# A 32 MB copy on 16 DMA engines: streams 1920 KB apart in place of 2 MB

## The chip, the core and the metric

The kernel runs on one core of one Trainium2 chip. The metric is the device time of the program in microseconds (us). A profile of one execution shows the span from the first to the last instruction, what each engine did in it, and the packets of the core's 16 DMA engines. In this text KB and MB in code and in address distances are 1024 and 1024 x 1024 bytes; MB and GB/s in the profile are decimal.

## The reference

```python
batch, seq, hidden, capacity = 16, 1024, 512, 256
x = randn(batch, seq, hidden)                      # float32, 32 MB
token_positions = randint(0, capacity, (batch, seq))

mask = token_positions < capacity
return (x * mask[..., np.newaxis]).astype(np.float32)
```

A row of 512 numbers is kept if its token's position is below the capacity, else it becomes zero. The positions are drawn below the capacity, so with these inputs every row is kept, and the output equals x. The kernel doesn't assume that: it tests the positions and has a branch for the other case.

## The kernel before

The kernel starts at once to copy x to out, from HBM to HBM, with transfers that SP (the sync engine) issues. The tensor is cut into 16 streams of 2 MB, one for each DMA engine. Each transfer takes the next stretch of every stream: 64 KB, then 192 KB, then seven times 256 KB.

```python
KB = 1024 // 4          # in float32 elements

x_e = x_b.rearrange("(e c) -> e c", e=16)
out_e = out_b.rearrange("(e c) -> e c", e=16)
c = 64 * KB
at = 0
for n in [1, 3] + [4] * 7:
    sp.dma_start(
        out=out_e[:, at : at + n * c], in_=x_e[:, at : at + n * c]
    ).then_inc(s_copy, 16)
    at += n * c
    n_copy += 1
```

Beside the copy, the positions are loaded through ACT's queue; the vector engine (DVE) compares them with the capacity, a matmul on TensorE (PE) adds up the kept rows of all partitions, and one more comparison gives a flag.

```python
act.dma_start(out=tp, in_=tp_i32.rearrange("(p w) -> p w", p=P)).then_inc(s_tp, 16)
# ... five DVE instructions: ge, lt, low, keep, kept ...
pe.matmul(out=total, lhsT=ones, rhs=kept, start=True, stop=True).then_inc(s_pe, 1)
ve.tensor_scalar(out=drop_i, in0=total, scalar1=float(N) - 0.5,
                 scalar2=None, op0=Alu.is_lt).then_inc(s_ve, 1)
```

If the flag says that a row is to be dropped, a branch multiplies x by the mask tile by tile and writes out again, after the copy is done. With these inputs the branch isn't taken. The last instruction of SP waits until all the transfers have landed:

```python
with nc.If(drop):
    ...                                   # not taken with these inputs
sp.wait_ge(s_copy, 16 * n_copy)
```

Of the kernel before, what the change touches and what calls it, by code (L numbers as in the profile page):

```python
# [1 line left out]

# [4 lines left out]


@with_exitstack
def kernel(  # L10
    ctx: ExitStack,
    tc: tile.TileContext,
    x: bass.AP,
    token_positions: bass.AP,
    capacity: bass.AP,
    out: bass.AP,
):
    nc = tc.nc
    P = nc.NUM_PARTITIONS
    fp32 = mybir.dt.float32  # L20
    i32 = mybir.dt.int32
    Alu = mybir.AluOpType

    x_f = x.flatten_outer_dims()
    out_f = out.flatten_outer_dims()
    N, D = x_f.shape
    n_per_p = N // P
    cap = float(int(capacity))
    x_r = x_f.rearrange("(p n) d -> p n d", p=P)
    out_r = out_f.rearrange("(p n) d -> p n d", p=P)  # L30
    tp_i32 = token_positions.rearrange("b s -> (b s)").bitcast(i32)

    sp = nc.sync
    act = nc.scalar
    ve = nc.vector
    pe = nc.tensor

    pool = ctx.enter_context(tc.tile_pool(name="mask", bufs=1))
    psum_pool = ctx.enter_context(tc.tile_pool(name="psum", bufs=1, space=bass.MemoryType.PSUM))
    tp = pool.tile([P, 2 * n_per_p], i32, name="tp")  # L40
    ge = pool.tile([P, n_per_p], fp32, name="ge")
    lt = pool.tile([P, n_per_p], fp32, name="lt")
    low = pool.tile([P, n_per_p], fp32, name="low")
    keep = pool.tile([P, n_per_p], fp32, name="keep")
    kept = pool.tile([P, 1], fp32, name="kept")
    ones = pool.tile([P, 1], fp32, name="ones")
    total = psum_pool.tile([1, 1], fp32, name="total")
    drop_i = pool.tile([1, 1], i32, name="drop_i")
    F = 16
    NBUF = 2  # L50
    n_fix = n_per_p // F
    xts = [pool.tile([P, F, D], fp32, name=f"xt{b}") for b in range(NBUF)]

    s_copy = tc.alloc_semaphore("s_copy")
    s_tp = tc.alloc_semaphore("s_tp")
    s_ve = tc.alloc_semaphore("s_ve")
    s_pe = tc.alloc_semaphore("s_pe")
    s_ld = [tc.alloc_semaphore(f"s_ld{b}") for b in range(NBUF)]
    s_mul = tc.alloc_semaphore("s_mul")
    s_st = [tc.alloc_semaphore(f"s_st{b}") for b in range(NBUF)]  # L60

    with tc.tile_critical():  # L62

        n_copy = 0
        x_b = x_f.rearrange("r d -> (r d)")
        out_b = out_f.rearrange("r d -> (r d)")

        def copy(eng, first, count, view, **sizes):
            eng.dma_start(
                out=out_b[first : first + count].rearrange(view, **sizes),  # L70
                in_=x_b[first : first + count].rearrange(view, **sizes),
            ).then_inc(s_copy, 16)

        KB = 1024 // 4
        MB = 1024 * KB

        x_e = x_b.rearrange("(e c) -> e c", e=16)
        out_e = out_b.rearrange("(e c) -> e c", e=16)
        c = 64 * KB
        at = 0  # L80
        for n in [1, 3] + [4] * 7:
            sp.dma_start(
                out=out_e[:, at : at + n * c], in_=x_e[:, at : at + n * c]
            ).then_inc(s_copy, 16)
            at += n * c
            n_copy += 1
        assert 16 * at == N * D


        act.dma_start(out=tp, in_=tp_i32.rearrange("(p w) -> p w", p=P)).then_inc(s_tp, 16)  # L90
        lo = tp[:, 0 : 2 * n_per_p : 2]
        hi = tp[:, 1 : 2 * n_per_p : 2]


        ve.memset(ones, 1.0).then_inc(s_ve, 1)  # L95
        ve.wait_ge(s_tp, 16)
        ve.tensor_scalar(  # L97
            out=ge, in0=lo, scalar1=0.0, scalar2=None, op0=Alu.is_ge
        ).then_inc(s_ve, 1)
        ve.wait_ge(s_ve, 2)  # L100
        ve.scalar_tensor_tensor(  # L101
            out=lt, in0=lo, scalar=cap, in1=ge, op0=Alu.is_lt, op1=Alu.mult
        ).then_inc(s_ve, 1)
        ve.wait_ge(s_ve, 3)
        ve.scalar_tensor_tensor(  # L105
            out=low, in0=hi, scalar=0.0, in1=lt, op0=Alu.is_equal, op1=Alu.mult
        ).then_inc(s_ve, 1)
        ve.wait_ge(s_ve, 4)
        ve.scalar_tensor_tensor(  # L109
            out=keep, in0=hi, scalar=0.0, in1=low, op0=Alu.is_lt, op1=Alu.add  # L110
        ).then_inc(s_ve, 1)
        ve.wait_ge(s_ve, 5)
        ve.tensor_reduce(  # L113
            out=kept, in_=keep, axis=mybir.AxisListType.X, op=Alu.add
        ).then_inc(s_ve, 1)
        pe.wait_ge(s_ve, 6)
        pe.matmul(out=total, lhsT=ones, rhs=kept, start=True, stop=True).then_inc(s_pe, 1)  # L117
        ve.wait_ge(s_pe, 1)
        ve.tensor_scalar(  # L119
            out=drop_i, in0=total, scalar1=float(N) - 0.5, scalar2=None, op0=Alu.is_lt  # L120
        ).then_inc(s_ve, 1)


        for e in (sp, act, ve):
            e.wait_ge(s_ve, 7)
        ET = mybir.EngineType
        drop = nc.values_load(
            drop_i[0:1, 0:1],
            engines=[ET.SP, ET.Activation, ET.DVE],
            min_val=0,  # L130
            max_val=1,
            skip_runtime_bounds_check_because="a comparison gives 0 or 1",
        )
        with nc.If(drop):
            for u in range(n_fix):
                b = u % NBUF
                if u >= NBUF:
                    sp.wait_ge(s_st[b], 16 * (u // NBUF))
                sp.dma_start(out=xts[b], in_=x_r[:, u * F : (u + 1) * F, :]).then_inc(s_ld[b], 16)
                ve.wait_ge(s_ld[b], 16 * (u // NBUF + 1))  # L140
                for j in range(F):
                    c = u * F + j
                    ve.tensor_scalar(
                        out=xts[b][:, j, :],
                        in0=xts[b][:, j, :],
                        scalar1=keep[:, c : c + 1],
                        scalar2=None,
                        op0=Alu.mult,
                    ).then_inc(s_mul, 1)
                if u == 0:  # L150
                    act.wait_ge(s_copy, 16 * n_copy)
                act.wait_ge(s_mul, (u + 1) * F)
                act.dma_start(out=out_r[:, u * F : (u + 1) * F, :], in_=xts[b]).then_inc(s_st[b], 16)
            for b in range(NBUF):
                act.wait_ge(s_st[b], 16 * (n_fix // NBUF))
        sp.wait_ge(s_copy, 16 * n_copy)


# [1 line left out]
_INS = ['x', 'token_positions', 'capacity']  # L160
_OUTS = [((16, 1024, 512), 'float32')]

_NUMBERS = {'capacity': 256}


# [26 lines left out]
```

## Time and profile before

| | |
|---|---|
| time, median of 2 runs | 172.03 us (170.79 to 173.28) |
| span in the profile | 170.1 us |
| busy time of DVE, the busiest compute engine | 1.6 us |
| moved by the copy | 33.55 MB read, 33.55 MB written |
| transfers of the copy | 9, in packets of 64 KB |

A packet is a piece that one DMA engine moves[...]; the profile gives the number of packets of each queue, their bytes, and the time that they took as a share of what 16 engines have in the span. Queue q1 carries the transfers that SP issued, q10 those of ACT. A view of windows gives the mean busy share of the 16 engines and the bytes moved, stretch by stretch. Each transfer ends with one small completion packet on each engine that took part; these count in the number of packets.

### The profile page before, as it was taken

What the parts mean: (1) busy time and instruction counts of PE and PEld (TensorE: products, weight loads), DVE (VectorE), ACT (ScalarE), POOL (GpSimd) and SP (SyncE); (2) the same over time, 40 slices, a digit from 0 to 9 for tenths busy, and PEclk for the clock granted to TensorE, in tenths of its full rate; (3) what the DMA queues carried; (4) which work ended last, traced back from release to release, by engine and by line L of the source; (5) the groups of instructions that cost most, each with busy time, mean ns of one, the idle gap of its engine ahead of it and who ended that gap; (6) DMA issues with size and microseconds to landing.
All of it is one profiled execution on the core that took longest, in us unless ns stands there. A gap on an engine that the chain in (4) does not pass through costs nothing. (4 is left out here: it accounts for less than half of the span.)

```text
span 170.1 us, 82 instructions
## 1 busy us (share of the span) xinstructions
PE 0.2 (0%) x2; PEld 0.1 (0%) x2; DVE 1.6 (1%) x7; POOL 0.2 (0%) x4
## 2 busy tenths in 40 slices
PE   0000000000000000000000000000000000000000
PEld 0000000000000000000000000000000000000000
DVE  2100000000000000000000000000000000000000
POOL 0000000000000000000000000000000000000000
DMA  9949999879999949999969999979999499999570
GB/s 277 200 92 216 233 247 231 185 154 185 231 247 247 216 92 231 200 247 231 185 123 216 231 247 200 200 154 200 231 247 231 92 216 200 247 247 231 108 154 0
DMA packets 801, 33.69 MB, mean 198 GB/s; under 512 B 160, under 2 KB 288, under 8 KB 288
## 3 DMA queue, kind: packets, MB, share of 16 engines
q1 hardware_dynamic: 656, 33.56, 96.4%
q10 hardware_dynamic: 144, 0.13, 0.2%
q14 instruction: 1, 0.01, 0.0%
HBM read 33.69 MB, written 33.55 MB: 395 GB/s over the span
## 5 line engine op out<-in xcount | busy, mean ns | idle before, releaser
L101 DVE SCALAR_TENSOR_TENSOR lt<-tp,ge 128x128 f32<-128x128 int32 x1 | 0.3, 293 | 0.0
L109 DVE SCALAR_TENSOR_TENSOR keep<-tp,low 128x128 f32<-128x128 int32 x1 | 0.3, 293 | 0.0
L105 DVE SCALAR_TENSOR_TENSOR low<-tp,lt 128x128 f32<-128x128 int32 x1 | 0.3, 291 | 0.0
L113 DVE TENSOR_REDUCE kept<-keep 128x1 f32<-128x128 f32 x1 | 0.3, 286 | 0.0
L97 DVE TENSOR_SCALAR ge<-tp 128x128 f32<-128x128 int32 x1 | 0.2, 226 | 2.0 <-DMA tp<-in_token_positions_dram 2.0
L117 PE MATMUL total<-kept,ones 128*1 128x1 f32 x2 | 0.2, 164 | 4.6 <-DVE kept L113 4.6
L119 DVE TENSOR_SCALAR drop_i<-total 1x1 int32<-1x1 f32 x1 | 0.1, 147 | 0.3 <-PE total L117 0.3
L173 POOL MEMSET const-uint8-127<- 128x1 uint8 x1 | 0.1, 103 | 0.0
L173 POOL MEMSET const-bfloat16-1.0<- 128x1 bf16 x1 | 0.1, 101 | 0.0
L173 POOL MEMSET const-float32-0.0<- 128x1 f32 x1 | 0.1, 98 | 0.2 <-issue 0.2
L173 POOL MEMSET const-float32-1.0<- 128x1 f32 x1 | 0.1, 98 | 0.0
L117 PEld LDWEIGHTS total<-kept,ones 128*1 128x1 f32 x2 | 0.1, 80 | 4.6 <-DVE kept L113 4.6
L95 DVE MEMSET ones<- 128x1 f32 x1 | 0.1, 59 | 1.0 <-SPq L62 1.0
## 6 DMA issues: line engine op xcount, KB each, us to landing
out_dram<-in_x_dram SPq DMA_DIRECT2D x9, 82.2
tp<-in_token_positions_dram ACTq DMA_DIRECT2D x1, 128.0 KB, 2.1
```

Of the source, the lines that this page charges most:

```text
L95: ve.memset(ones, 1.0).then_inc(s_ve, 1)
L97: ve.tensor_scalar(out=ge, in0=lo, scalar1=0.0, scalar2=None, op0=Alu.is_ge).then_inc(s_ve, 1)
L101: ve.scalar_tensor_tensor(out=lt, in0=lo, scalar=cap, in1=ge, op0=Alu.is_lt, op1=Alu.mult).then_inc(s_ve, 1)
L105: ve.scalar_tensor_tensor(out=low, in0=hi, scalar=0.0, in1=lt, op0=Alu.is_equal, op1=Alu.mult).then_inc(s_ve, 1)
L109: ve.scalar_tensor_tensor(out=keep, in0=hi, scalar=0.0, in1=low, op0=Alu.is_lt, op1=Alu.add).then_inc(s_ve, 1)
L113: ve.tensor_reduce(out=kept, in_=keep, axis=mybir.AxisListType.X, op=Alu.add).then_inc(s_ve, 1)
L117: pe.matmul(out=total, lhsT=ones, rhs=kept, start=True, stop=True).then_inc(s_pe, 1)
L119: ve.tensor_scalar(out=drop_i, in0=total, scalar1=float(N) - 0.5, scalar2=None, op0=Alu.is_lt).then_inc(s_ve, 1)
L173: nc = _bacc.Bacc("TRN2", target_bir_lowering=False, num_devices=1)
```

## The change

The 16 streams start 1920 KB apart, where they were 2 MB apart, and each is 1920 KB long. They cover the first 30 MB of the tensor: 64 KB, 192 KB, six times 256 KB, and 128 KB of each stream. The last 2 MB of the tensor are copied by one further transfer, again cut into 16 parts, of 128 KB each. What it is for: DMA engines that start together and move at the same pace stand at equal offsets within their streams, so their addresses differ by multiples of the streams' distance; another distance gives other combinations of addresses in HBM at any moment.

```diff
-        x_e = x_b.rearrange("(e c) -> e c", e=16)
-        out_e = out_b.rearrange("(e c) -> e c", e=16)
-        c = 64 * KB
+        E = 16
+        PITCH = 1920 * KB
+        x_e = x_b[0 : E * PITCH].rearrange("(e c) -> e c", e=E)
+        out_e = out_b[0 : E * PITCH].rearrange("(e c) -> e c", e=E)
         at = 0
-        for n in [1, 3] + [4] * 7:
+        for c in [64, 3 * 64] + [4 * 64] * 6 + [2 * 64]:
             sp.dma_start(
-                out=out_e[:, at : at + n * c], in_=x_e[:, at : at + n * c]
+                out=out_e[:, at : at + c * KB], in_=x_e[:, at : at + c * KB]
             ).then_inc(s_copy, 16)
-            at += n * c
+            at += c * KB
             n_copy += 1
-        assert 16 * at == N * D
+        assert at == PITCH
+        copy(sp, E * PITCH, N * D - E * PITCH, "(e c) -> e c", e=E)
+        n_copy += 1
```

The function `copy` issues one transfer of a stretch of x to the same stretch of out and lets it add 16 to `s_copy`. As built, the last transfer has 32 rows of 64 KB.

## The prediction

> **What bounds the kernel now.** I read the page from its top: first the line of busy times, to see whether any engine computes for a noticeable part of the span; then the queues; then the waits of the queue that issues the copies; and last the rate in windows of 10 us, because a mean over the span hides its ends.
>
> The head of the page and the part on DMA queues:
>
> ```profile
> span 170.1 us, 82 instructions
> PE 0.2 (0%) x2; PEld 0.1 (0%) x2; DVE 1.6 (1%) x7; POOL 0.2 (0%) x4
> ...
> q1 hardware_dynamic: 656, 33.56, 96.4%
> q10 hardware_dynamic: 144, 0.13, 0.2%
> ...
> HBM read 33.69 MB, written 33.55 MB: 395 GB/s over the span
> ```
>
> No compute engine is busy for more than 1.6 us of 170.1. The queue q1, which SP feeds, holds packets on the 16 DMA engines for 96.4% of the span. So the copy from x to out is the kernel. The 656 packets of q1 can be checked: 32 MB in pieces of 64 KB are 512, and 9 transfers with one completion packet on each of 16 engines are 144; 512 + 144 = 656. So every transfer does use 16 engines, and each engine moves 512 / 16 = 32 pieces.
>
> Next the waits of SP's queue (who waited, for whom, how long in total, how often, the longest), and the copies' issues in the merged timeline (start, duration, engine, line):
>
> ```profile
> SPq L156 <- DMA out_dram<-in_x_dram: 160.6, 1, 160.6
> ...
> 0.95 6.37 SPq L82 DMA_DIRECT2D out_dram<-in_x_dram  x9
> ...
> 4.83 0.15 DVE L119 TENSOR_SCALAR drop_i<-total 1x1 int32<-1x1 f32 x1 [0.28 <-PE total L117]
> ```
>
> All nine transfers are issued between 0.95 and 7.32 us, after that SP waits 160.6 us for their bytes. The test of the mask is over at 4.98 us, under the first pieces of the copy. The view of the chain that ended last lists only these first 5 us and a DMA share of 1%: it follows the mask back and doesn't show the copy, so it is not the view to read here; the 160.6 us wait is.
>
> Then the windows (stretch, length, four engines' busy time, granted clock, mean DMA share, GB/s written), the first, three from the middle and the last:
>
> ```profile
> 0.00:10.00 10.00, 0.19 (x2) 0.09 (x2) 1.59 (x7) 0.20 (x4) 1.00 1.06 223
> ...
> 60.00:70.00 10.00, 0.00 (x0) 0.00 (x0) 0.00 (x0) 0.00 (x0) 1.00 1.06 216
> 70.00:80.00 10.00, 0.00 (x0) 0.00 (x0) 0.00 (x0) 0.00 (x0) 1.00 0.90 184
> 80.00:90.00 10.00, 0.00 (x0) 0.00 (x0) 0.00 (x0) 0.00 (x0) 1.00 0.85 164
> ...
> 160.00:171.00 11.00, 0.00 (x0) 0.00 (x0) 0.00 (x0) 0.00 (x0) 1.00 0.45 89
> ```
>
> The fifteen windows from 10 to 160 us read 211, 210, 203, 210, 210, 216, 184, 164, 203, 210, 203, 197, 216, 203, 210; they sum to 3050, so the mean is **203.3 GB/s** (a packet is counted whole in one window, so single values jump). At that rate 33.55 MB take 33.55 / 0.2033 = 165.0 us. The remaining 170.1 - 165.0 = 5.1 us are what doesn't depend on the rate: the first data packet starts at 2.4 us by the packet records of the trace, and the rest is the uneven finish of the engines (the sixteen completions of the last transfer come at 165.1 to 168.8 us) and the closing of the program. The median time is 172.03, that is 1.9 us above the span. So **time = 7.0 us + 33.55 MB / rate**, and the change can act on the rate alone.
>
> One more reading, from the packet records: one 64 KB piece took 5.12 us on average, with 3.61 as the shortest and 6.69 as the longest. The shortest, in the first round, is 18.2 GB/s for one engine, and 16 times that would be 290 GB/s. Hence one engine by itself can go faster than the 12.8 GB/s (65,536 bytes / 5.12 us) that it gets; what holds it back seems to be something that the 16 share. That is the opening for a change of addresses.
>
> **What the Trainium skill says.** DMA: Bandwidth & Descriptors, section Latency and other measured facts, has a row on the pitch of HBM rows: copies between HBM tensors in tiles of 128 rows of 16 KiB ran at 207 GB/s with rows 512 KiB apart, 164 with 2 MiB, 103 with 4 and 8 MiB, and 214 ("full") with 4 MiB padded by 4 KiB. It calls channel aliasing of streams in lock-step an inference. Does the trace agree? Streams here are 2 MB apart and yet reach 203.3, not 164: either few streams suffer less than 128 rows, or the neighbours in time on that page are the first rows of each engine's share. If an engine takes 8 neighbouring rows, its stream there starts 8 x 512 KiB = 4 MiB from the next engine's in the 207 case and 16 MiB in the 164 case; a spacing of 2 MB would then lie on the good side of 207. The trace's 203.3 fits this second reading, which is my choice.
>
> HBM Reference, section Specifications, says that a core alone measures about 425 GB/s. Reads and writes together, the trace has 2 x 203.3 = 407 GB/s in the steady part. If that figure holds for the sum of both directions, which no run here shows, there is room for 425 / 407 = 1.045.
>
> DMA: Bandwidth & Descriptors, section on why a DMA increments its semaphore by 16, says that the number of engines is the largest divisor up to 16 of the slowest dimension. The 656 packets agree for a dimension of 16. The new last transfer is built as 32 rows of 64 KB, which 16 divides, so it should use 16 engines too, with two pieces each.
>
> **The change part by part.**
> 1. *Pieces and bytes.* Before: 1 + 3 + 7 x 4 = 32 pieces of 64 KB for each engine. After: 1 + 3 + 6 x 4 + 2 = 30, which is 1920 KB, and 2 from the last transfer: again 32. No packet gets smaller. 0 us.
> 2. *One transfer more.* Ten in place of nine: 16 completion packets more, one per engine; each lasts 9 ns in the packet records. One issue more on SP: 6.37 / 9 = 0.71 us, at about 7.3 us, when the first transfers keep the engines occupied to 25.1 us (last completion of the second). Hidden. Together under 0.05 us.
> 3. *Mask, branch, PE, DVE.* Same instructions, over at 5 us. 0 us.
> 4. *The order of addresses.* At any moment the engines stand at one offset inside their streams, give or take. Before, the sixteen addresses are equal except in multiples of 2 MB. After, 1920 KB = 2 MB - 128 KB, so each stands 128 KB further back within its 2 MB block, and sixteen engines stand at sixteen different multiples of 128 KB. This is the whole purpose, and covers 30 of 32 pieces; in the last two the streams are 128 KB apart. It doesn't separate anything below 128 KB.
>
> So the sum is 7.0 + 33.55 / rate. Rate 203.3 (nothing gained): 7.0 + 165.0 = 172.0. Rate 207: 7.0 + 162.1 = 169.1. Rate 214 (the page's "full"): 7.0 + 156.8 = 163.8. All are estimates from the formula of the trace and the named page.
>
> **The rivals.**
> *A: the 2 MB spacing costs nothing today, and the time stays.* For it: 203.3 GB/s is not far from the page's 207 and far from 164; and the engines are not in exact lock-step. In every round the sixteen starts lie about 3 us apart, which at 12.8 GB/s is 38 KB of address, more than the 4 KiB that cured the case on the page. So the streams may be spread already. Against it: the short first-round piece shows a shared limit, and the pieces scatter from 3.6 to 6.7 us. Time 171 to 173.
> *B: the streams do collide now, and part of the gap to 214 is recovered.* For it: the page's row, and 5.0% between 203.3 and 214. Against: the same drift of 38 KB. Time 164 to 168.5.
> *C: the new spacing collides more.* No trace or page shows which address bits choose a channel; 1920 KB is still a multiple of 128 KB, and sixteen addresses that move one field up while another goes down may fall together as well as apart. A rate of 195 would give 7.0 + 172.1 = 179. Against: nothing here makes this spacing look special.
> *D: a tail.* The last 2 MB could land unevenly or on fewer engines. With 32 rows it shouldn't; two pieces per engine are 10 us of the end whichever way they are addressed. Worth 1 us at most.
>
> **Range and chances.** I give A a half, B somewhat more than a third, C an eighth or so. The middle of that mixture is just below the time before: 170.3 us. The range runs from nearly full recovery, 164.5, to a slight loss, 175.0. The 2% limits stand at 168.6 and 175.5; B lies mostly below the first, C partly above the second: faster 0.35, same 0.53, slower 0.12.
>
> **What would show each step.** The page after should have q1 with 512 + 160 = 672 packets and the same 33.56 MB; more data packets would break step 1. The issue group of SP should still end by 9 us, with the mask over at 5. Windows from 10 to 160 us near 203 mean A; 207 to 214 in all of them mean B; below 200 C. If the middle windows rise and the last 10 us get slower, D took it back. The formula itself is wrong if the time moves by more than the windows say. The prediction fails upward if the spacing makes collisions that it didn't have, downward if the shared limit was the collision and the ceiling is above the page's 214.

## The result, and the profile after

The changed kernel takes **108.84 us** (median of 2 runs, 108.81 to 108.86) against 172.03: a ratio of 0.633, 95% interval 0.613 to 0.652. That is far below the predicted range; the time fell by 63 us.

Lines of the page after, in the same order as those shown of before: span and busy engines, queues, bytes.

```profile
span 107.0 us, 83 instructions
PE 0.2 (0%) x2; PEld 0.1 (0%) x2; DVE 1.6 (1%) x7; POOL 0.2 (0%) x4
...
q1 hardware_dynamic: 672, 33.56, 95.5%
...
HBM read 33.69 MB, written 33.55 MB: 628 GB/s over the span
```

The same bytes, 512 data packets and 10 x 16 completion packets, the same 1.6 us of DVE, and the DMA engines as fully occupied as before (95.5% against 96.4%). That share says nothing of how fast the packets move: it adds up the times that packets took, however long each one lasts. The figure that moved is the last one, 395 to 628 GB/s (read and written together).

SP's waits and issues after, in the order of before:

```profile
SPq L159 <- DMA out_dram<-in_x_dram: 97.4, 1, 97.4
```

```profile
0.95 5.87 SPq L83 DMA_DIRECT2D out_dram<-in_x_dram  x9
6.87 0.59 SPq L69 DMA_DIRECT2D out_dram<-in_x_dram  x1
```

The tenth issue ends at 7.46 us, hidden as expected. The wait for the bytes is 97.4 us where it was 160.6: a difference of 63.2 us, the whole gain. The windows (stretch, length, busy times, clock, DMA share, GB/s written), and last the mean over the middle:

```profile
0.00:10.00 10.00, 0.19 (x2) 0.09 (x2) 1.59 (x7) 0.20 (x4) 1.00 1.00 328
...
60.00:70.00 10.00, 0.00 (x0) 0.00 (x0) 0.00 (x0) 0.00 (x0) 1.00 1.08 354
70.00:80.00 10.00, 0.00 (x0) 0.00 (x0) 0.00 (x0) 0.00 (x0) 1.00 0.96 315
80.00:90.00 10.00, 0.00 (x0) 0.00 (x0) 0.00 (x0) 0.00 (x0) 1.00 1.02 334
...
100.00:108.00 8.00, 0.00 (x0) 0.00 (x0) 0.00 (x0) 0.00 (x0) 1.00 0.37 131
10.00:100.00 90.00, 0.00 (x0) 0.00 (x0) 0.00 (x0) 0.00 (x0) 1.00 1.00 326
```

The copy is faster in every window, from the first on; nothing is special to the end. Over 10 to 100 us the mean is 326 GB/s, where it was 203. In the packet records one 64 KB piece takes 3.19 us on average where it took 5.12. So the question is not where in the kernel the time went, but why the same piece on the same engine took 1.9 us longer with streams 2 MB apart.

### The profile page after: what moved, and what is told of

It reads as the page before. It is cut to its first block, busy times and chain, and to the rows that moved or that the text cites. A ratio compares the mean times of both kernels' runs of the same rounds, so it can differ in the third digit from the quotient of the medians.

```text
span 107.0 us, 83 instructions
## 1 busy us (share of the span) xinstructions
PE 0.2 (0%) x2; PEld 0.1 (0%) x2; DVE 1.6 (1%) x7; POOL 0.2 (0%) x4
## 3 DMA queue, kind: packets, MB, share of 16 engines
q1 hardware_dynamic: 672, 33.56, 95.5%
HBM read 33.69 MB, written 33.55 MB: 628 GB/s over the span
```

## The experiments

The theory after the result: streams that stand at the same place within a 2 MB block hinder each other, and what counts is over how many places the sixteen are spread. Most experiments replace the copy by **stages**, so that several distances can be compared in one run with the same pieces of 64 KB. Such a kernel copies only part of out, and parts of it several times; its total time is no measure, its stages are. The mask part stays as it was. In outline:

```diff
-        for c in [64, 3 * 64] + [4 * 64] * 6 + [2 * 64]:
-            sp.dma_start(out=out_e[:, ...], in_=x_e[:, ...]).then_inc(s_copy, 16)
+        for E, read_pitch, write_pitch in [...]:        # one stage each
+            for j in range(8):                          # E pieces of 64 KB per transfer
+                sp.dma_start(out=rows(out_b, E, write_pitch, j),
+                             in_=rows(x_b, E, read_pitch, j)).then_inc(s_copy, 16)
+                n_copy += 1
+            sp.wait_ge(s_copy, 16 * n_copy)             # a stage lands before the next starts
```

A stage of 16 streams moves 8.39 MB. Each window below runs from the first packet of a stage to its last; its second figure is the length, the last one the GB/s. "Piece" is the mean time of one 64 KB packet, from the packet records. Each stage was executed once in its run, but two of them stand in four runs: 16 streams at 2048 KB gave 193 to 198 GB/s, and at 1920 KB 320 to 328. Differences of that size between the windows of single stages mean nothing; the pieces of these stages agree better, 5.13 to 5.18 and 3.13 to 3.15 us.

### Distances that are powers of two

> The copy is replaced by seven stages, each of eight transfers of one 64 KB piece for each of 16 streams, and SP waits for a stage to land before it starts the next; only part of out is written. Streams 2048, 1024, 512, 256, 128, 64 and 1920 KB apart, in this order. Theory A (streams that agree in all address bits below 2 MB collide; what counts is how many different places within a 2 MB block the sixteen take: 1, 2, 4, 8, 16, 16, 16): time of eight pieces 41 us at 2048, between 30 and 40 at 1024, near 26 from 512 down and at 1920. Rival B (every power of two is bad, 1920 KB is good because it is not one): 41 us in six stages, 26 only in the last. Rival C (the gain lies in the shape of the whole copy, not in the distance): all seven alike.

Windows of the stages 2048, 1024, 512, 256, 128, 64 and 1920 KB, in this order:

```profile
2.40:45.80 43.40, 0.19 (x2) 0.09 (x2) 1.54 (x6) 0.00 (x0) 1.00 0.95 193
47.40:78.90 31.50, 0.00 (x0) 0.00 (x0) 0.00 (x0) 0.00 (x0) 1.00 0.97 266
80.40:106.80 26.40, 0.00 (x0) 0.00 (x0) 0.00 (x0) 0.00 (x0) 1.00 0.97 318
108.40:133.90 25.50, 0.00 (x0) 0.00 (x0) 0.00 (x0) 0.00 (x0) 1.00 0.97 329
135.40:160.80 25.40, 0.00 (x0) 0.00 (x0) 0.00 (x0) 0.00 (x0) 1.00 0.98 330
162.40:188.10 25.70, 0.00 (x0) 0.00 (x0) 0.00 (x0) 0.00 (x0) 1.00 0.97 326
189.70:215.30 25.60, 0.00 (x0) 0.00 (x0) 0.00 (x0) 0.00 (x0) 1.00 0.98 328
```

One place (2048 KB): 193 GB/s. Two places: 266. Four: 318. Eight and sixteen: 326 to 330, as much as 1920 KB. The pieces go from 5.18 us over 3.79 and 3.19 to 3.09. Powers of two are not bad as such, and the stages, whose transfers are all alike in shape, show the whole difference by distance alone: this run's rivals B and C fall.

### Distances a little below 2 MB

> Same stages of eight pieces for each of 16 streams, streams 2048, 2047, 2044, 2040, 2032, 2016, 1984 and 1920 KB apart. Theory fine (a difference of a few KB between streams is enough; what the drift of 38 KB seemed to give already): 41 us at 2048, 26 us from 2044 on. Theory coarse (only address bits of tens of KB and more separate the streams, which is why the drift did not help): 41 us down to 2040 or 2032, then falling, 26 us at 1984 and 1920.

Stages 2048, 2047, 2044, 2040, 2032, 2016, 1984 and 1920 KB:

```profile
2.30:45.10 42.80, 0.19 (x2) 0.09 (x2) 1.53 (x6) 0.00 (x0) 1.00 0.97 197
46.70:87.20 40.50, 0.00 (x0) 0.00 (x0) 0.00 (x0) 0.00 (x0) 1.00 0.97 207
88.70:122.40 33.70, 0.00 (x0) 0.00 (x0) 0.00 (x0) 0.00 (x0) 1.00 0.96 249
124.00:154.90 30.90, 0.00 (x0) 0.00 (x0) 0.00 (x0) 0.00 (x0) 1.00 0.97 271
156.50:184.80 28.30, 0.00 (x0) 0.00 (x0) 0.00 (x0) 0.00 (x0) 1.00 0.96 296
186.40:212.80 26.40, 0.00 (x0) 0.00 (x0) 0.00 (x0) 0.00 (x0) 1.00 0.97 318
214.40:240.60 26.20, 0.00 (x0) 0.00 (x0) 0.00 (x0) 0.00 (x0) 1.00 0.95 320
242.10:268.30 26.20, 0.00 (x0) 0.00 (x0) 0.00 (x0) 0.00 (x0) 1.00 0.96 320
```

Neither expectation holds as it stood. There is no step, neither at a few KB nor at tens of KB: the rate climbs gradually, 197, 207, 249, 271, 296, 318, and stays at 320. Put in terms of how wide the sixteen are spread (15 times the difference from 2 MB): 15 KB brings almost nothing, 60 KB about two fifths of the gain, 120 KB as much as two places (266), 480 KB as much as four (318). A place has no sharp edge, then: a spread of some tens of KB still costs more than two separate places do.

### Reads and writes apart

> Five stages of eight pieces for 16 streams; the distance of the read streams and of the written streams is set separately (out is then a permuted and partial copy): read 2048 and write 2048; read 1920 and write 2048; read 2048 and write 1920; both 1920; both 2048 with the writes shifted by 960 KB against the reads. Theory R (the reads collide): 41, 26, 41, 26, 41 us. Theory W (the writes collide): 41, 41, 26, 26, 41. Theory RW (each side collides in itself): 41, 35 to 41, 35 to 41, 26, 41. Theory X (a stream's write collides with its own read at the same offset): 41, 26, 26, 26 or 41, 26.

```profile
2.40:45.20 42.80, 0.19 (x2) 0.09 (x2) 1.53 (x6) 0.00 (x0) 1.00 0.97 197
46.70:81.70 35.00, 0.00 (x0) 0.00 (x0) 0.00 (x0) 0.00 (x0) 1.00 0.96 240
83.20:116.10 32.90, 0.00 (x0) 0.00 (x0) 0.00 (x0) 0.00 (x0) 1.00 0.96 255
117.70:143.50 25.80, 0.00 (x0) 0.00 (x0) 0.00 (x0) 0.00 (x0) 1.00 0.98 325
145.10:187.00 41.90, 0.00 (x0) 0.00 (x0) 0.00 (x0) 0.00 (x0) 1.00 0.96 200
```

Spreading the reads alone (second line) or the writes alone (third) gives each about half the gain; only both give 325. In pieces: 3.15 us with both spread, 3.94 with the reads at 2 MB, 4.20 with the writes at 2 MB, 5.15 with both. The extras of 0.79 and 1.05 add up to 1.84 of the 2.00 seen together, so the two sides are nearly independent. Shifting all the writes by 960 KB against the reads (last line) changes little, 200 GB/s for 197, so it is not a stream's write that collides with its own read. Theory RW has the pattern, though the stage with the writes spread came out shorter, 32.9 us, than the 35 to 41 it said.

### How many engines it takes

> Eight stages of eight 64 KB pieces on 2, 4, 8 and 16 engines, at each number first with streams 2048 KB apart and then 1920; only part of out is written. Theory shared collision: with 2 engines both distances take the same, about 8 x 2.5 to 3 us; the 2048 KB stages grow with the number of engines and reach 41 us at 16, while those of 1920 KB stay flat up to 8 and reach 26 at 16. Rival (an engine by itself is slow at this distance, for a reason that doesn't depend on the others): 2048 KB is 41 us at every number.

The last four stages: 8 engines at 2048 and at 1920 KB, 16 engines at 2048 and at 1920.

```profile
91.70:112.30 20.60, 0.00 (x0) 0.00 (x0) 0.00 (x0) 0.00 (x0) 1.00 0.48 204
113.90:134.30 20.40, 0.00 (x0) 0.00 (x0) 0.00 (x0) 0.00 (x0) 1.00 0.49 206
135.90:178.20 42.30, 0.00 (x0) 0.00 (x0) 0.00 (x0) 0.00 (x0) 1.00 0.97 198
179.70:205.50 25.80, 0.00 (x0) 0.00 (x0) 0.00 (x0) 0.00 (x0) 1.00 0.98 325
```

This is the most telling run. Up to eight engines it makes no difference whether the distance is 2048 or 1920 KB: a piece takes 2.49 to 2.60 us in the mean on 2, 4 or 8 engines, never less than 2.418. The expectation had the 2048 KB stages grow with the number of engines; up to eight they don't. Eight engines copied 204 GB/s with streams 2 MB apart; sixteen copied 198. By these two windows, half of the engines of the kernel before added nothing.

### Farther distances and other numbers of streams

> Eight stages of eight 64 KB pieces for each stream, part of out only: 8 streams 2048 KB apart; 8 at 4096; 4 at 8192; 2 at 16384; 12 at 2048; 12 at 1920; 16 at 1536; 16 at 1023 KB. Theory places (streams that stand at the same place within 2 MB share about 200 GB/s of copy, an engine alone does 2.42 us for a piece, and 16 well-spread streams about 3.1): mean piece 2.45 us for the first four; 12 x 64 KB / 204 = 3.85 at 12 streams and 2048 KB, 2.45 to 2.6 at 1920; 1536 KB gives four places and so 3.2 us as 512 KB did; 1023 KB gives two clusters a few KB wide, so 3.5 to 3.8. Rival (bits above 2 MB spread the streams as well, and farther is worse): 8 at 4096 takes clearly over 2.5 us, 4 at 8192 too. Rival (round distances are bad, odd ones good): 1536 and 1023 KB both 3.1.

Pieces: 8 streams at 2048 KB 2.58 us, 8 at 4096 2.94, 4 at 8192 2.50, 2 at 16384 2.54, 12 at 2048 3.09, 12 at 1920 2.52, 16 at 1536 3.23, 16 at 1023 3.89. The stages of 12 streams, and of 1536 and 1023 KB:

```profile
98.40:125.10 26.70, 0.00 (x0) 0.00 (x0) 0.00 (x0) 0.00 (x0) 1.00 0.70 236
126.90:147.60 20.70, 0.00 (x0) 0.00 (x0) 0.00 (x0) 0.00 (x0) 1.00 0.73 304
149.20:175.70 26.50, 0.00 (x0) 0.00 (x0) 0.00 (x0) 0.00 (x0) 1.00 0.98 317
177.30:209.10 31.80, 0.00 (x0) 0.00 (x0) 0.00 (x0) 0.00 (x0) 1.00 0.98 264
```

1536 KB is no power of two, but its multiples take only four places within 2 MB, and it gives 317 GB/s, as 512 KB did (318). 1023 KB is as odd as can be and gives 264, as two places did (266). For 16 streams the rule of places holds, that of round and odd numbers falls. But one part of the theory fell here: that colliding streams share a constant 204 GB/s. Twelve of them should then take 3.85 us a piece and took 3.09. And 8 streams at 4096 KB were slower than at 2048, which could have been chance. Four streams at 8192 KB were not slowed. The next run was for the number of streams and for the 4096 KB.

> Eight stages of eight 64 KB pieces for each stream, part of out only: 8 streams at 2048 KB; 8 at 4096; 10, 12 and 14 at 2048; again 8 at 4096 and 8 at 2048; 14 at 1920. Theory constant cap (colliding streams share about 204 GB/s whatever their number): mean piece 2.6, 3.2, 3.85, 4.5 us at 8, 10, 12, 14. Theory crowding (each further stream at the same place lowers the total): about 2.5, 2.6 to 2.8, 3.1, 3.8 to 4.3. The 4096 KB stages: 2.9 both times if bits above 2 MB matter, 2.45 to 2.6 if the 2.94 seen once was chance. 14 at 1920: 2.65 to 2.9, between the engines' own 2.42 and the 3.1 of sixteen.

| streams, distance | piece, us | streams x 64 KB / piece, GB/s |
|---|---|---|
| 8, 2048 KB | 2.53 and 2.49 | 208 and 210 |
| 8, 4096 KB | 2.92 and 2.89 | 179 and 181 |
| 10, 2048 KB | 2.67 | 245 |
| 12, 2048 KB | 3.08 | 255 |
| 14, 2048 KB | 3.66 | 251 |
| 14, 1920 KB | 2.82 | 325 |
| 16, 2048 KB (other runs) | 5.13 to 5.18 | 202 to 205 |

The windows of 10, 12 and 14 streams at 2048 KB, which also contain the end of a stage, when some engines have finished:

```profile
51.60:74.00 22.40, 0.00 (x0) 0.00 (x0) 0.00 (x0) 0.00 (x0) 1.00 0.60 234
75.80:102.30 26.50, 0.00 (x0) 0.00 (x0) 0.00 (x0) 0.00 (x0) 1.00 0.70 237
104.00:135.70 31.70, 0.00 (x0) 0.00 (x0) 0.00 (x0) 0.00 (x0) 1.00 0.81 232
```

By the pieces the total is about 250 from 10 to 14 streams, and down to 202 to 205 at 16. Colliding streams do crowd each other, but not along the line that I wrote down (3.8 to 4.3 us at 14). Why the last two streams cost so much is open. The 4096 KB stages are slower both times: bits above 2 MB have some effect too.

Nor does each place have a limit of its own. At 1024 KB the sixteen stand eight and eight at two places, and a piece takes 3.79 us; eight at one place, with no others beside them, took 2.49. So a limit per place does not account for what is seen; what does is open.

### Whole copies

Three whole copies that write all of out, each executed four times, and the changed kernel again beside two of them. In outline (out is cut as x is):

```diff
# f256: blocks of 4 MB, 16 streams 256 KB apart (block 0 in two transfers, of one piece and of three)
+        x_e = x_b.rearrange("(b e c) -> e b c", e=16, c=256 * KB)
+        for at in range(1, 8):
+            sp.dma_start(out=out_e[:, at : at + 1, :], in_=x_e[:, at : at + 1, :])
# f128: blocks of 2 MB, 16 streams 128 KB apart, first all first halves, then all second
+        x_e = x_b.rearrange("(b e h c) -> h e b c", e=16, h=2, c=64 * KB)
# pad4k: the changed kernel with another distance; the last 64 KB by one more transfer
-        PITCH = 1920 * KB
+        PITCH = 2044 * KB
-        for c in [64, 3 * 64] + [4 * 64] * 6 + [2 * 64]:
+        for c in [64, 3 * 64] + [4 * 64] * 6 + [3 * 64, 60]:
```

> The whole copy in blocks of 4 MB, each cut into 16 streams of 256 KB, same 64 KB pieces, nine transfers, so nothing at 2 MB and no odd distance. Theory places: as fast as the changed kernel or a little faster: 32 pieces of 3.1 us are 99, and 6 us more: 105 to 109 us. Rival (only 1920 KB with its separate last transfer brings the gain): near 172.

> The whole copy in blocks of 2 MB, each cut into 16 streams of 128 KB, of which first the first 64 KB of all blocks are copied, then the second; within a stream pieces lie 2 MB apart, streams never. Theory places: 105 to 109 us. Rival (a 2 MB step inside one engine's own list of pieces hurts too): over 115.

> The changed kernel itself on the same chip as the two whole copies beside it, for comparison with them. Expected 108.8 us, with the mean piece at 3.19.

> The whole copy with streams 2044 KB apart, which is what a pad of 4 KB amounts to, and the last 64 KB by one more transfer. From the stage at that distance, 4.04 us a piece: 32 x 4.04 + 6 = 135 us. If a few KB were enough: 108 us. If the stage was too short to show that the streams lock together again: up to 172.

| whole copy | median, us | lowest to highest | ratio to before, 95% interval |
|---|---|---|---|
| before, beside the next three | 172.12 | 172.03 to 174.59 | |
| changed kernel again | 108.50 | 108.22 to 108.97 | 0.628 (0.620 to 0.637) |
| f256 | 106.97 | 106.83 to 107.52 | 0.618 (0.610 to 0.627) |
| f128 | 107.03 | 106.98 to 107.35 | 0.620 (0.611 to 0.628) |
| before, beside pad4k | 172.44 | 171.06 to 173.23 | |
| pad4k | 136.92 | 136.19 to 137.42 | 0.790 (0.778 to 0.802) |

The table leaves out slow executions (over 1.5% above the fastest of the same kernel): four of seven of before in either row, and one of pad4k, 138.52 us. f256 and f128 have neither 1920 KB nor a separate end, and are a little faster than the changed kernel: by 1.5 us, 1.4%, with ranges over four runs that don't touch. What these 1.5 us are made of is not shown. Their mean piece is 3.13 us against 3.17. f128 steps 2 MB from block to block within each engine's list: such steps in time cost nothing, only streams at one place at the same moment do. The windows of pad4k and of f256 over their middle:

```profile
10.00:120.00 110.00, 0.00 (x0) 0.00 (x0) 0.00 (x0) 0.00 (x0) 1.00 1.00 257
```

```profile
10.00:100.00 90.00, 0.00 (x0) 0.00 (x0) 0.00 (x0) 0.00 (x0) 1.00 1.00 335
```

A pad of 4 KB gives 257 GB/s in the whole kernel as in the stage (249), 137 us where the stage foretold 135. The gain is real, but it leaves 30 us.

## Why the prediction was wrong

**What was right.** The bound (the copy, with everything else hidden), parts 1 to 3 (672 packets, the issue at 7 us, the mask over at 5) and the form of the sum. With the measured rate the formula gives 7.0 + 33.55 / 0.326 = 109.9 us, against 108.84. Its term "rate" was wrong: 195 (rival C) to 214 was allowed for, 326 came. The prediction's rival B named the mechanism, with somewhat more than a third of the weight, and its last sentence named the way it would fail: "if the shared limit was the collision and the ceiling is above the page's 214". C and D didn't happen (the last transfer's two pieces per engine took 5.9 us, from 99.2 to 105.1 by the means of the completions).

**The step that failed first: the ceiling.** The prediction took 214 GB/s, "full" in the Trainium skill's page DMA: Bandwidth & Descriptors (section Latency and other measured facts), for what a copy without collisions reaches, and 425 in HBM Reference (section Specifications (TRN2)) for the sum of both directions. Neither is a ceiling here: 16 spread streams copy 326 to 335 GB/s, which is 652 to 670 in both directions. The page's 207, 164 and 103 still rightly say that distance matters; its level is not that of this kernel. Because 203.3 lay near 207, the prediction chose the reading in which a spacing of 2 MB "would then lie on the good side of 207", and so at most 5% were to be had. But 203.3 was no sign of an unhindered copy: e4 copied as much, 204, with half of the engines.

The profile had spoken against it, and the prediction had read it: the shortest piece, 3.61 us, made 290 GB/s if all sixteen could do it. That figure was nearer to the 326 that came than the 214 taken from the page. On 2 to 8 engines the piece is in fact 2.42 us at its shortest, 27.1 GB/s for one engine; at 5.12 us each engine ran at under half of that.

**The second step that failed: the drift.** Rival A, which got half of the weight, held that starts 3 us apart (1.4 to 3.5 us, round by round), 38 KB of address, might already spread the streams. The gain shows that they did not do so enough. How little such a spread is worth is read from the near distances, for no run took the drift itself away: there 15 KB raise 197 to 207, 60 KB to 249, and 480 KB give 318. The comparison with "the 4 KiB that cured the case on the page" took the pad of one stream for the spread of all: sixteen streams with 4 KB each are 60 KB wide. And even that recovered here only two fifths of the rate, as pad4k confirms (257, between 203 and 335).

**What is shown and what not.** Shown: the gain is the rate of the pieces; it comes from the places that the streams take within 2 MB; reads and writes each collide among themselves; and it depends on how many streams run, since eight in all are not slowed at 2 MB, ten hardly (2.67 us) and sixteen by 2.0 us a piece. Not shown: which part of HBM or of the way to it is the place (a channel, a bank, something in between), why 16 streams lose so much against 14, why eight at one place are slowed by eight at another, and what the address bits above 2 MB do.

**What bounds the kernel now** is again something that the engines share: at 1920 KB the mean piece takes 2.50 us with 8 streams, 2.52 with 12, 2.82 with 14 and 3.14 with 16, so that the total by the pieces goes 210, 312, 325, 334 and levels off. What it is, is not shown. HBM Reference (section Specifications (TRN2)) gives about 716 GB/s for a stack, shared by two cores; 2 x 335 = 670 is, as an estimate by that figure, 94% of it. That would fit, but no run here tests it.

## What to carry to other kernels

When many DMA streams copy from HBM to HBM side by side, choose their distance so that at any moment they stand at many different places within 2 MB (here, sixteen places 32 KB apart gave 318 GB/s, 64 KB and more 320 to 330); neighbouring stretches, in blocks that move along together, do this with no padding: stretches of 128 and 256 KB were the fastest whole copies here, and one of 64 KB was as fast in its stage. A DMA share of 96% says that packets were nearly always under way, not that they moved as fast as they can: divide bytes by the time of one packet, and compare with the shortest packet in the trace or with the same transfer on half the engines. If half the engines are as fast as all, they are held by something that they share, and here that was the addresses.

## What the runs showed of the hardware that I had not expected

One DMA engine copies 64 KB from HBM to HBM in 2.418 us at its shortest (27.1 GB/s), and in 2.49 to 2.60 us in the mean, while up to seven others do the same, at 2048 or 1920 KB. By the mean pieces, sixteen streams 2 MB apart copy 202 to 205 GB/s, eight of them 203 to 211, twelve 254 to 255. Sixteen spread streams copied 335 GB/s over 90 us of a whole kernel. Eight streams 4 MB apart are about 15% slower per piece than eight 2 MB apart (2.89 to 2.94 us against 2.49 to 2.58), although both stand at one place within 2 MB.
